# Block 2: projections woven with solve and scan together, hyena's two orders with the linear attention, its rows kept in SBUF, and the loop for large decays ahead of the solve

## The chip, the cores and the metric

The kernel runs on one NeuronCore of a Trainium2 chip. The core has a matrix engine (PE, with its weight loads as PEld), a vector engine (DVE), a scalar engine (ACT), GpSimd (POOL) and SyncE (SP), whose queue starts nearly all transfers here. Each engine works through its own instructions in order and waits for the others by semaphores. The metric is the device time of one execution in microseconds (us); the lower the better.

## What is computed

Two transformer blocks over one batch of 512 tokens of width 1024, in float32. Block 1 (RWKV-7 in both directions, neighbourhood attention, a mixture of experts) is not touched by the change. Block 2 takes block 1's output x and runs a mixer of three kinds of heads side by side, then an output projection and an MLP:

```python
def mixer(h, hc, ...):
    zl_hy, zl_gla, zl_gdn = split_last(h @ w_in, IN_SIZES)     # latent, 512 tokens
    zc_hy, zc_gla, zc_gdn = split_last(hc @ w_in, IN_SIZES)    # context, 256 tokens
    hy_lat = hyena_mix(zl_hy, ...)          # two long convolutions by FFT, each with a gate
    gla_lat, gla_ctx = gla_branch(zl_gla, zc_gla, ...)         # gated linear attention
    gdn_lat, gdn_ctx = gdn_branch(zl_gdn, zc_gdn, ...)         # gated delta rule
    y_lat = jnp.concatenate([hy_lat, gla_lat, gdn_lat], axis=-1) @ w_out

def hyena_mix(...):
    y = v
    for o, gate in enumerate((x1, x2)):
        conv = irfft(rfft(y, n=2 * l) * filt_f[None, :, o], n=2 * l)[:, :l]
        y = gate * (conv + d_skip[o] * y)

def gla_chunk_scan(q, k, v, log_a, s0):     # per chunk of 64 tokens
    b = jnp.cumsum(ac, axis=2)
    attn = einsum('bhid,bhjd,bhijd->bhij', qc, kc, exp(where(mask, b_i - b_j, -inf)))
    o = (qc * exp(b)) @ s + attn @ vc
    s_new = exp(b_last) * s + (kc * exp(b_last - b)).T @ vc

def gdn_chunk_scan(q, k, v, g, beta, s0):   # per chunk of 64 tokens
    a = -(kb @ kc.T) * exp(where(strict, diff, -inf))
    w, u = triangular_solve(eye - a, [kb * exp(gcum), vc * bc])
    v_new = u - w @ s
    o = (qc * exp(gcum)) @ s + attn @ v_new
    s_new = exp(g_last) * s + (kc * exp(g_last - gcum)).T @ v_new
```

Both scans run forward and backward over eight chunks of 64 tokens, four heads each, and the two directions are added. Each head's rows are then normalised (`gated_head_norm`), multiplied by a gate and go into the output projection. The context's part of the mixer is computed earlier in the kernel and leaves the starting states of the two scans.

## The kernel before

**Number format.** A float32 product is made of three matmuls on numbers split into a high and a low part: `mm3` (L293 to L295) issues high x high, low x high, high x low. The split is an ACT copy (L839, or L287 for weights) and a DVE subtraction (L840, L288).

**Weaving.** The order of the program is written by generators. `weave` (L331) takes streams with a weight each; a stream yields the cost of the piece that it has just written, and the stream with the least cost over weight writes next. A higher weight thus gives a stream more of the program for each piece of the others. All engines' instruction orders follow from it, through a scheduler that may move an instruction ahead where its inputs and buffers allow.

**Block 2's mixer, `mixer_in`.** In the order of the program:

- *Early.* `side_proj` (its loop at L1899) is a stream of projections of the latent: for each block of 128 columns 24 matmuls `gps` of 128x512 (8 pieces of the width, three each), then a store to DRAM. Its first nine blocks (`GDN_BLOCKS`: q, k, v of the delta rule) are written in `early()`, woven with `prep()`, which reads them back and lays them out, and with `gla_flags`, which finds whether any decay of the linear attention is too large for the fast form.
- *Solve.* `gdn_solve` makes, for each of two pairs of heads, decays and products (`dps`, `kkp`, `qkp`), and inverts the chunks' triangular matrices (`inverse`: a sum F to DRAM and back as n16, fifteen steps on DVE, to DRAM and back as qc, masked to qv, then 128 small matmuls `ips` and the result TQ). It is woven with all that is left of `side`, the other 20 blocks, weights 64 and 108. The projections' buffers are then given up (`far.close`).
- *Scan.* `gdn_scan` has eight chunks, one behind the other. In a chunk, for each head: `gxp` (key times state), gX on DVE, `gup` (TQ times gX), vd on DVE and vn on ACT, `gsp` (key times vd), the new state gSn on DVE; and the output `gop` with Og on ACT and DVE, stored to `ogd`. It is woven, 128 to 48, with `hy_tables` (loads and splits the DFT's tables) and `hyena(hp, 0)`: transposes `hyt`, forward DFT `dfp` (96 matmuls of 128x256 for an order), the filter's product on DVE and POOL, inverse DFT `hip` (48 matmuls of 128x512), and hv on DVE.
- *The loop for large decays.* `gla_general` reads the flag into registers (`TENSOR_LOAD aflag`, L1683) and runs its body 0 or 1 times; with the given data it is skipped. It would write the rows to `oad`, which else hold zeros.
- *Last stage.* `gla` is woven, 112 to 36 to 40, with the head norm of the delta rule's rows (`head_norm_out` on `ogd`) and `hyena(hp, 1)`, whose hv go to `mixd` in DRAM. For each chunk and pair of heads `gla` makes the output `aop` and the state's `asp`; the output is added to a piece of `oad` that is read into the tile Oa and written back (L1636 to L1638).

**`mixer_out`** begins with the head norm of `oad` (eight loads hO, `ops` that adds the directions, `otp` transposes), woven with `side()`: two blocks of hyena and three of the delta rule are read from `mixd` (`uld`), split into vh, vl and uh, ul, and multiplied with the output weights (`gpt`). The linear attention's three blocks come last.

## Time and profile before

| | us |
|---|---|
| median of 3 runs | 2232.9 |
| lowest and highest | 2223.94, 2236.71 |
| profiled execution | 2231.45 |
| its span | 2229.7 |
| mean granted clock of PE | 0.925 of full speed |

| engine | busy us | share of the span | instructions |
|---|---|---|---|
| PE | 1979.0 | 89% | 15280 |
| DVE | 1141.5 | 51% | 2542 |
| ACT | 718.0 | 32% | 1390 |
| POOL | 241.8 | 11% | 246 |

The stages that the change touches lie between about 1290 and 1845 us of the span: the early stage until 1417.5, the solve until 1537.3, the scan until 1654.8, the loop's stop until 1661.0, the last stage until 1756.5 (the last `aop`), the gap to the first `gpt` at 1778.8, then the output projection. All else is equal in both programs. Busy times are read by stage; a busy PE is not PE at its peak, since its matmuls overlap and get longer when the granted clock is low.

### The profile page before, as it was taken

To read this page: it belongs to the slowest core of one execution; us is meant where nothing else is said; L and a number is where in the kernel's file an instruction comes from. 1 tells how busy PE (TensorE), PEld (TensorE's weight loads), DVE (VectorE), ACT (ScalarE), POOL (GpSimd) and SP (SyncE) were. 2 spreads that over 40 slices of the span, in tenths; PEclk is the share of its full clock that TensorE was granted. 3 is DMA by queue.
4 is the path that set the end of the run, shared out by engine and by line. 5 is a ranking of instruction groups with operands and counts; after the bars stand their busy time and mean duration, and the time that the engine had idled before them with its cause. 6 is when DMAs were issued, how large, how long until landed. Compare 5 with 4: busy or idle time off the path is not lost. (4 is left out here: it accounts for less than half of the span.)

```text
span 2229.7 us, 37859 instructions
## 1 busy us (share of the span) xinstructions
PE 1979.0 (89%) x15280; PEld 1445.7 (65%) x15280; DVE 1141.5 (51%) x2542; ACT 718.0 (32%) x1390; POOL 241.8 (11%) x246
## 2 busy tenths in 40 slices
PE   7999999989688789999999487999989788999997
PEld 5777777657565675444534265776666486899897
DVE  4655555542136545454361487656547475433433
ACT  4333332312126343121322455423223124312321
POOL 0010000010000201111000031210001050000000
PEclk9999999986889988999999798998789799999998
DMA  5343222462555438978687432333123532333332
GB/s 152 105 99 106 63 87 56 129 188 87 187 173 174 156 113 294 315 299 291 256 312 261 170 113 89 101 107 114 39 66 119 169 107 91 92 96 92 94 94 76
DMA packets 183028, 319.54 MB, mean 143 GB/s; under 512 B 77896, under 2 KB 99161, under 8 KB 182843
## 3 DMA queue, kind: packets, MB, share of 16 engines
q1 hardware_dynamic: 175354, 303.38, 42.6%
q0 software_dynamic: 4608, 8.40, 1.1%
q10 hardware_dynamic: 2880, 5.24, 0.8%
q8 instruction: 122, 2.00, 0.4%
q14 instruction: 64, 0.52, 0.1%
HBM read 281.90 MB, written 43.44 MB: 146 GB/s over the span
## 5 line engine op out<-in xcount | busy, mean ns | idle before, releaser
L288 DVE TENSOR_TENSOR wl<-wraw,wh 128x1024 fp32r<-128x1024 f32 (+2 forms) x215 | 223.3, 1040 | 202.8 <-ACT wh L287 202.3
L287 ACT ACTIVATE wh<-wraw 128x1024 fp32r<-128x1024 f32 (+2 forms) x233 | 195.7, 844 | 284.4 <-PE gpt L326 149.1
L293 PE MATMUL gps<-hh,wh 128*128 128x512 f32 x568 | 234.1, 413 | 0.4 <-DVE rS L380 0.4
L295 PE MATMUL gps<-hl,wh 128*128 128x512 f32 x568 | 229.7, 405 | 0.0
L294 PE MATMUL gps<-hh,wl 128*128 128x512 f32 x568 | 229.1, 404 | 0.3 <-DVE wl L288 0.3
L1170 PE MATMUL hps<-w,xT 128*64 128x512 f32 x512 | 142.0, 612 | 1.7 <-DMA w<-in_w_moe 1.5
L324 PE MATMUL gpt<-wh,mh 128*128 128x256 f32 x512 | 142.9, 279 | 0.0
L325 PE MATMUL gpt<-wl,mh 128*128 128x256 f32 x512 | 142.9, 279 | 0.0
L326 PE MATMUL gpt<-wh,ml 128*128 128x256 f32 x512 | 142.9, 279 | 0.0
L293 PEld LDWEIGHTS gps<-hh,wh 128*128 128x128 f32 x568 | 108.2, 191 | 29.4 <-issue 3.9
L295 PEld LDWEIGHTS gps<-hl,wh 128*128 128x128 f32 x568 | 107.8, 190 | 25.1 <-issue 0.9
L294 PEld LDWEIGHTS gps<-hh,wl 128*128 128x128 f32 x568 | 108.0, 190 | 24.4 <-DVE wl L288 0.7
L294 PE MATMUL gps<-lhh,wl 128*128 128x512 f32 x232 | 96.8, 419 | 9.1 <-DVE wl L288 7.5
L293 PE MATMUL gps<-lhh,wh 128*128 128x512 f32 x232 | 95.7, 414 | 6.5 <-ACT cpad L1262 4.6
L325 PEld LDWEIGHTS gpt<-wl,mh 128*128 128x128 f32 x512 | 96.2, 188 | 0.1
L324 PEld LDWEIGHTS gpt<-wh,mh 128*128 128x128 f32 x512 | 96.2, 188 | 0.1
L326 PEld LDWEIGHTS gpt<-wh,ml 128*128 128x128 f32 x512 | 96.2, 188 | 0.0
L295 PE MATMUL gps<-lhl,wh 128*128 128x512 f32 x232 | 95.1, 412 | 0.2 <-DVE lhl L275 0.2
L1996 POOL TENSOR_TENSOR x<-x,xev 128x512 f32<-128x512 f32 x36 | 49.9, 1393 | 409.4 <-DVE xev L1994 406.4
L1170 PEld LDWEIGHTS hps<-w,xT 128*64 128x64 f32 x512 | 37.2, 138 | 64.0 <-issue 52.3
L324 PE MATMUL gpt<-wh,uh 128*128 128x256 f32 x224 | 66.1, 295 | 5.6 <-ACT wh L287 2.1
L1271 DVE SCALAR_TENSOR_TENSOR cout<-cpad,cw,cout 128x512 f32<-128x512 f32 (+1 forms) x90 | 68.6, 762 | 2.0
(1176 smaller groups left out, 4251.2 us busy)
## 6 DMA issues: line engine op xcount, KB each, us to landing
w<-in_w_moe SPq DMA_DIRECT2D x192, 512.0 KB
wraw<-in_w_modb SPq DMA_DIRECT2D x48, 512.0 KB
wraw<-in_w_in_2b SPq DMA_DIRECT2D x41, 512.0 KB
wraw<-in_w_inb SPq DMA_DIRECT2D x39, 512.0 KB
wraw<-in_w_mlp1b SPq DMA_DIRECT2D x32, 512.0 KB
wraw<-in_w_mlp2b SPq DMA_DIRECT2D x32, 512.0 KB
gd<-st SPq DMA_DIRECT2D x16, 256.0 KB
bm<-in_c_bias SPq DMA_DIRECT2D x16, 256.0 KB
```

The source lines that it names most:

```text
L287: nc.scalar.activation(wh, raw[:, o:o + g], AF.Copy)
L288: self.we.tensor_sub(wl, raw[:, o:o + g], wh)
L293: nc.tensor.matmul(ps, wh, hh, start=first, stop=False)
L294: nc.tensor.matmul(ps, wl, hh, start=False, stop=False)
L295: nc.tensor.matmul(ps, wh, hl, start=False, stop=last)
L324: nc.tensor.matmul(ps, hh[:, g, sl], wh[:, k], start=f, stop=False, skip_group_check=True)
L325: nc.tensor.matmul(ps, hh[:, g, sl], wl[:, k], start=False, stop=False, skip_group_check=True)
L326: nc.tensor.matmul(ps, hl[:, g, sl], wh[:, k], start=False, stop=l, skip_group_check=True)
L1170: nc.tensor.matmul(ps[q], xT[:, 4 * kh + k, q], self.parts[h][:, 512 * (k - 2 * c):512 * (k - 2 * c) + 512], start=kh == 0 and k == 0, sto ...
L1271: nc.vector.scalar_tensor_tensor(ov[:n], pv[:n, :, j:j + L], wcol[:n, j:j + 1], ov[:n], op0=OP.mult, op1=OP.add)
L1996: (nc.gpsimd if last is None or cb < 3 else nc.vector).tensor_add(o, o, t)
```

## The change

- `gla` adds its outputs to a slice of a tile that stays in SBUF, `self.oa` (1.5 MB), which is filled once from `oad` ahead of the stage. The 16 loads of Oa, the 16 stores, and the eight loads hO of the second head norm are gone. The tile's pool, `self.ox`, is closed in `mixer_out`, behind the head norm.
- `early()` runs through 16 blocks (the nine of the delta rule and seven of the linear attention) with weight 96 in place of nine with 54.
- `gla_general` stands right behind that, ahead of the solve.
- Solve and scan are one stream, `chain()`, woven 192 to 66 with the rest of the projections.
- `hy_tables`, both orders of hyena, `gla` and the delta rule's head norm are woven in one stage, 88 to 112 to 36; nothing of hyena is woven with the scan.

```diff
@@ -1632,10 +1632,8 @@
                             hh = 2 * hp + h
                             nc.tensor.matmul(op[t, h, :], attn[h][t, c, :], v[t, c, 96 * hh:96 * hh + 96], start=False, stop=h == 1,
                                              skip_group_check=True)
-                    O = pool.tile([128, 192], F32, name="Oa", bufs=3)
-                    nc.sync.dma_start(O, od[c, :, 192 * hp:192 * hp + 192])
+                    O = od[:, c, 192 * hp:192 * hp + 192]
                     nc.vector.tensor_add(O, O, op.rearrange("p h d -> p (h d)"))
-                    nc.sync.dma_start(od[c, :, 192 * hp:192 * hp + 192], O)
                 if c < S - 1 or ctx:
                     for z in range(2):
 
@@ -1921,7 +1919,7 @@
             self.there.add(n)
             yield 6
 
-    def head_norm_out(self, pool, od, gate, gcol, j0):
+    def head_norm_out(self, pool, od, gate, gcol, j0, O=None):
 
         nc, C = self.nc, self.C
         sgs = []
@@ -1930,9 +1928,10 @@
             nc.sync.dma_start(sg, self.sgd[gate + j])
             sgs.append(sg)
         yt = pool.tile([128, 4, 4, 96], F32, name="hyt")
-        O = pool.tile([128, 8, 384], F32, name="hO")
-        for c in (0, 7, 1, 6, 2, 5, 3, 4):
-            nc.sync.dma_start(O[:, c], od[c])
+        if O is None:
+            O = pool.tile([128, 8, 384], F32, name="hO")
+            for c in (0, 7, 1, 6, 2, 5, 3, 4):
+                nc.sync.dma_start(O[:, c], od[c])
         ss = pool.tile([128, 4, 4], F32, name="hss")
         for tt in range(4):
             ps = self.ps.tile([128, 384], F32, name="ops", tag="p", bufs=2)
@@ -2077,7 +2076,7 @@
 
         nc = self.nc
         tp = self.tc.tile_pool
-        self.far = ExitStack()
+        self.far, self.ox = ExitStack(), ExitStack()
         w = self.w = self.view(dict(p="g", s="g", i="p"), wg=512)
         cx, w.wraw, w.wsp = [self.far.enter_context(tp(name=n, bufs=b, side="right"))
                                    for n, b in (("lat", 1), ("wr3", 2), ("ws3", 2))]
@@ -2124,37 +2123,40 @@
                             st[hp] = yield from v.gdn_kv(hp, 8, gd, gt, src, hp)
 
                 def early():
-                    while not w.there.issuperset(GDN_BLOCKS):
+                    while not w.there.issuperset(SIDE_BLOCKS[:16]):
                         yield next(side)
                 with tp(name="gf", bufs=1) as gf:
-                    self.run(self.weave((early(), 54), (prep(), 60), (v.gla_flags(8, gf), 20)))
+                    self.run(self.weave((early(), 96), (prep(), 60), (v.gla_flags(8, gf), 20)))
+                with tp(name="gz", bufs=1) as ga:
+                    v.gla_general(8, ga, lambda n: load(ga, self.gpd[n], "lsc"), self.oad)
 
                 with tp(name="gs", bufs=1) as gs, tp(name="rp2", bufs=1) as v.rp:
                     heads = []
 
-                    def solve():
+                    def chain():
                         with tp(name="gs2", bufs=1) as tmp, tp(name="ri2", bufs=1) as v.ri:
                             for hp in range(2):
                                 kv, kT = st[hp]
                                 E, TQ = yield from v.gdn_solve(hp, 8, gs, tmp, st["g"], kT, st["q"], hp)
                                 heads.extend((2 * hp + e, kT[:, e], st["q"][:, 2 * hp + e], kv[:, :, e], kv[:, :, 2 + e], E[:, e], TQ[e])
                                              for e in range(2))
+                        yield from v.gdn_scan(8, gs, heads, st["g"], self.ogd)
                     next(side)
-                    self.run(self.weave((solve(), 64), (side, 108)))
+                    self.run(self.weave((chain(), 192), (side, 66)))
                     self.far.close()
+                    self.oa = self.ox.enter_context(tp(name="oa", bufs=1, side="right")).tile([128, 8, 384], F32, name="oa")
+                    nc.sync.dma_start(self.oa, self.oad.rearrange("c p d -> p c d"))
                     hp = self.far.enter_context(tp(name="hy", bufs=1, side="right"))
                     u = self.view(dict(p="g", s="g", i="g"))
 
-                    def hyena0():
+                    def hyena():
                         yield from u.hy_tables(hp)
                         yield from u.hyena(hp, 0)
-                    self.run(self.weave((v.gdn_scan(8, gs, heads, st["g"], self.ogd), 128), (hyena0(), 48)))
-            with tp(name="gz", bufs=1) as ga:
-                v.gla_general(8, ga, lambda n: load(ga, self.gpd[n], "lsc"), self.oad)
+                        yield from u.hyena(hp, 1)
             with tp(name="ga", bufs=1) as ga, tp(name="hn", bufs=1) as hn:
                 un = self.view(dict(p="i"))
-                self.run(self.weave((v.gla(8, False, ga, lambda n: load(ga, self.gpd[n], "lsc"), self.oad), 112),
-                                    (un.head_norm_out(hn, self.ogd, 0, self.gng, 5), 36), (u.hyena(hp, 1), 40)))
+                self.run(self.weave((v.gla(8, False, ga, lambda n: load(ga, self.gpd[n], "lsc"), self.oa), 112),
+                                    (un.head_norm_out(hn, self.ogd, 0, self.gng, 5), 36), (hyena(), 88)))
             self.far.close()
 
     def mixer_out(self, xs, x, ev):
@@ -2181,7 +2183,8 @@
                     self.gemm_tm("w_out_2b", cb, uh[:, 3:], ul[:, 3:], 4, ev(cb), 1, 1, nk=3)
                     yield 4
             with tp(name="hn", bufs=1) as pool:
-                self.run(self.weave((self.head_norm_out(pool, self.oad, 3, self.agng, 2), 18), (side(), 28)))
+                self.run(self.weave((self.head_norm_out(pool, None, 3, self.agng, 2, self.oa), 18), (side(), 28)))
+            self.ox.close()
             for k in range(3):
                 take(2 + k, uh[:, k], ul[:, k])
             for cb in range(4):
```

What this does to the order of instructions, at the three places where most is moved:

PE, a chunk in the middle of the scan, before. kT, kv, TQ and E are keys, keys and values, inverses and products of the delta rule; dh, dl, di with hs0 and hs1 are hyena's tables and spectra:

```order
L294 MATMUL hip<-dh,hs0l 128x512
L295 MATMUL hip<-dl,hs0h 128x512
L1469 MATMUL gup<-gX,TQ_13339 64x96 x2
L293 MATMUL hip<-di,hs1h 128x512
L294 MATMUL hip<-di,hs1l 128x512
L295 MATMUL hip<-dl,hs1h 128x512
L293 MATMUL hip<-di,hs1h 128x512
L1469 MATMUL gup<-gX,TQ_13358 64x96 x2
L294 MATMUL hip<-di,hs1l 128x512
L1483 MATMUL gsp<-vd__14994,kv_12156 96x96
```

The same place after, a chunk late in the scan:

```order
L1494 MATMUL gop<-gSn,qT__12177 64x96 x4
L1459 MATMUL gxp<-gSn,kT_12863 64x96 x2
L1469 MATMUL gup<-gX,TQ_13841 64x96 x2
L1469 MATMUL gup<-gX,TQ_13860 64x96 x2
L1483 MATMUL gsp<-vd__14880,kv_12360 96x96 x2
L1469 MATMUL gup<-gX,TQ_14219 64x96 x2
L1496 MATMUL gop<-vn__14882,E_13484 64x96 x2
```

The 128x512 matmuls of hyena are gone from between the scan's own; no projections stand in their place here. Of all 696 `gps` matmuls 353 stand ahead of the solve's first matmul before and 444 after, 343 and 228 from there to the last `ips`, none and 24 behind it.

PE at the skipped loop, before: what stands ahead of it are hyena's forward DFTs of order 1.

```order
L293 MATMUL dfp<-yth,dh 128x256 x2
L294 MATMUL dfp<-yth,dl 128x256 x2
L295 MATMUL dfp<-ytl,dh 128x256 x2
L293 MATMUL dfp<-yth,dh 128x256
L1683 TENSOR_LOAD aflag
L1684 COMPARE_AND_BRANCH
```

After, at the end of the early stage; `tcp` are transposes of the preparation:

```order
L1373 MATMUL tcp<-ct_58,kv_12692 96x128 x8
L295 MATMUL gps<-lhl,wh 128x512
L293 MATMUL gps<-lhh,wh 128x512
L294 MATMUL gps<-lhh,wl 128x512
L295 MATMUL gps<-lhl,wh 128x512
L1681 TENSOR_LOAD aflag
L1682 COMPARE_AND_BRANCH
```

The branch moved from between scan and last stage to between early stage and solve.

SP's queue from the end of the last stage on, before: Oa and hO are the linear attention's rows, x the residual, uld what the output projection reads.

```order
L1636 DMA Oa<-oad 128x192 x2
L1935 DMA hO<-oad 128x384 x3
L1638 DMA oad<-Oa 128x192 x2
L1935 DMA hO<-oad 128x384
L225 DMA g1r<-mdd 128x1024
L1987 DMA x_16742<-x1d 128x1024 x4
L1935 DMA hO<-oad 128x384
L2170 DMA uld<-mixd 128x512 x2
```

The same place after; hsg are the gates of the head norm, wraw the output weights:

```order
L1885 DMA mixd<-hv_15572 128x512
L1885 DMA mixd<-hv_15573 128x512
L225 DMA g1r<-mdd 128x1024
L1986 DMA x_16699<-x1d 128x1024 x4
L1928 DMA hsg_16717<-sgd 128x512
L1928 DMA hsg_16719<-sgd 128x512
L1928 DMA hsg_16721<-sgd 128x512
L2172 DMA uld<-mixd 128x512 x2
```

The rows' reads and writes are gone, and hyena's last two stores now stand shortly ahead of the uld that reads them.

## Rows read from the trace of the kernel before

**Rows 1.** Busy time by stretch: start:end, us, each engine, PEclk, DMA share, GB/s.

```profile
1369.00:1398.00 29.00, 20.56 (x86) 15.19 (x87) 17.90 (x52) 18.05 (x34) 2.57 (x6) 0.82 0.37 118
1417.50:1537.30 119.80, 112.01 (x1136) 90.16 (x1134) 79.55 (x151) 29.46 (x51) 21.39 (x23) 0.98 0.36 100
1537.30:1654.80 117.50, 113.66 (x782) 76.56 (x781) 65.55 (x232) 36.23 (x104) 6.50 (x8) 0.77 0.19 60
1661.00:1756.50 95.50, 87.78 (x775) 65.42 (x776) 60.39 (x146) 29.30 (x55) 11.93 (x10) 0.87 0.38 119
1756.50:1778.80 22.30, 11.89 (x31) 3.53 (x30) 2.48 (x5) 4.08 (x9) 0.00 (x0) 0.77 0.73 254
...
1537.20:1546.85 9.65, 7.62 (x70) 4.92 (x66) 6.29 (x26) 2.65 (x8) 0.00 (x0) 0.90 0.74 222
```

In each of these rows the five busy times are those of PE, PEld, DVE, ACT and POOL, with the number of instructions.

**Rows 2.** Timeline of PE, two neighbouring projection matmuls: start, us, engine, line, operation.

```profile
1410.02 0.39 PE L294 MATMUL gps<-lhh,wl 128*128 128x512 f32 x1
1410.25 0.39 PE L295 MATMUL gps<-lhl,wh 128*128 128x512 f32 x1
```

**Rows 3.** Timeline of PE behind the skipped loop; idle time before it in brackets.

```profile
1661.01 0.58 PE L294 MATMUL dfp<-yth,dl 128*128 128x256 f32 x1 [5.58 <-issue]
```

**Rows 4.** The solve: PE's costliest group, then DVE's timeline.

```profile
L294 PE MATMUL gps<-lhh,wl 128*128 128x512 f32 x115 | 46.8, 407 | 4.8 <-DVE wl L288 4.8
...
1473.06 0.68 DVE L702 TENSOR_TENSOR TQ<-ips,qv 128x512 f32<-128x512 f32 x1
1492.06 1.07 DVE L649 TENSOR_REDUCE F<-Nw 128x128 f32<-128x512 f32 x1
1536.59 0.69 DVE L702 TENSOR_TENSOR TQ<-ips,qv 128x512 f32<-128x512 f32 x1 [0.24 <-PE ips L682]
```

**Rows 5.** Waits of DVE in the scan: us in total, times, longest.

```profile
DVE gSn L1486 <- PE gsp L1483: 24.9, 32, 2.7
```

**Rows 6.** The line of gxp: count, ns min/median/max, first and last start.

```profile
L1459 PE MATMUL gxp<-gSn,kT x112: 246/297/423, 1541.6 to 1648.8; 96*64 96x96 f32 x112
```

**Rows 7.** Timeline of DVE, the first gX of chunks 0 and 1.

```profile
1537.19 0.31 DVE L1462 TENSOR_SCALAR gX<-gxp,eG 128x96 f32<-128x96 f32 x1
1546.85 0.31 DVE L1462 TENSOR_SCALAR gX<-gxp,eG 128x96 f32<-128x96 f32 x1
```

**Rows 8.** Hyena: PE's timeline, DVE's groups in the scan, DVE's timeline.

```profile
1661.61 0.41 PE L293 MATMUL dfp<-yth,dh 128*128 128x256 f32 x1
1661.82 0.41 PE L294 MATMUL dfp<-yth,dl 128*128 128x256 f32 x1
...
1665.10 0.28 PE L294 MATMUL dfp<-yth,dl 128*128 128x256 f32 x1
1665.22 0.28 PE L295 MATMUL dfp<-ytl,dh 128*128 128x256 f32 x1
...
L840 DVE TENSOR_TENSOR dl<-hraw,dh 128x512 fp32r<-128x512 f32 x8 | 5.3, 683 | 0.8 <-ACT dh L839 0.8
L1885 DVE TENSOR_TENSOR hv<-hv,hx 128x512 f32<-128x512 f32 x2 | 1.4, 680 | 0.0
...
1647.53 0.68 DVE L1885 TENSOR_TENSOR hv<-hv,hx 128x512 f32<-128x512 f32 x1
1737.20 0.68 DVE L1885 TENSOR_TENSOR hv<-hv,hx 128x512 f32<-128x512 f32 x1
```

**Rows 9.** The gap: timelines of DVE and PE, then the chain: start, us, what.

```profile
1757.63 0.67 DVE L1637 TENSOR_TENSOR Oa<-Oa,aop 128x192 f32<-128x192 f32 x2 [2.20 <-DMA Oa<-oad]
1772.07 0.90 PE L1943 MATMUL ops<-hO,ct 128*64 128x384 f32 x1 [4.61 <-DMA hO<-oad]
1778.83 0.39 PE L324 MATMUL gpt<-wh,vh 128*128 128x256 f32 x1 [1.51 <-ACT wh L287]
...
1809.79 4.90 DMA uld<-mixd
1819.92 3.27 DMA uld<-mixd
```

## Prediction

> **What bounds the kernel now.** I read the busy time by stage first [rows 1], because the share of busy time over the whole span mixes stages with different limits. The change touches five stages of block 2, and the reader should see in [rows 1] that each has its own limit. The tail of the early stage (1369.0 to 1398.0 us) is loose: PE works 20.56 of 29.00 us, at a granted clock of 0.82. The solve (1417.5 to 1537.3) is PE's: 112.01 of 119.80 us busy at 0.98, DVE only 79.55. The scan (1537.3 to 1654.8) looks like PE's too, 113.66 of 117.50, but at a clock of 0.77: its matmuls take long, and hyena's large ones stand among the scan's small ones. The last stage before the output projection (1661.0 to 1756.5) has PE at 87.78 of 95.50. The gap behind it (1756.5 to 1778.8) is a wait for memory: PE 11.89 of 22.30, DVE 2.48.
>
> Then the waits of DVE inside the scan [rows 5]: the state update gSn waits 24.9 us, 32 times, for its own matmul gsp. The scan is a serial chain PE, DVE, PE, DVE, and PE works in order. The instruction order of before shows hip matmuls between gup and gsp, so the chain's next matmul comes behind them. The rows of two gX [rows 7] show what a chunk costs where hyena is still thin: the first gX of chunk 0 starts at 1537.19, that of chunk 1 at 1546.85, so 9.66 us, against 117.5 / 8 = 14.7 us on the mean.
>
> The profiled execution took 2231.45 us, 1.45 less than the median of the runs shown. The sum is made against it, and 1.45 is added at the end.
>
> **Early stage: +11.** The instruction order has 353 projection matmuls (gps, of 696) ahead of the solve's first matmul before, and 444 after: 91 more. Two neighbours start 0.23 us apart [rows 2], so 91 x 0.23 = 20.9 us of PE work comes into this stage. The loose stretch has 29.00 - 20.56 = 8.4 us of idle PE in it, and a clock of 0.82; were it full, the 20.56 us of work there would take up to 3.7 less, of which I take 1.5. So 20.9 - 8.4 - 1.5 = +11. Bounds: 0, if the blocks spread under all of the preparation, and +20.9, if none of it is hidden.
>
> **Loop for large decays: 0.** Its body is skipped, but PE stood still 5.58 us for it [rows 3]; it now does so between the early stage and the solve. The instruction is the same and is taken once in both programs, and in both places PE has work waiting. Bounds: -5.6, if PE's projections and preparation run out under it, and +5.6, if the solve's start now waits for a second engine's branch. [...]
>
> **Solve: -26.** PE is the bound. It holds 344 projection matmuls now, three lines of 115 or so, one of which is the first row of [rows 4]; the order of after leaves 228 there (91 go ahead, 24 are woven with the scan). 115 or 116 fewer x 0.23 = 26.5 us. A look at the chain says the same can be had: from TQ of the first pair of heads (1473.06) to F of the second (1492.06) are 19.0 us [rows 4], in which the second pair's decays and products are made; after has both pairs' fronts at the stage's start, and of the 19 I leave 4 for Nw and F, a saving of 15, and the inverse's 128 ips matmuls stand in a row where gps lay between them (44.5 us from F to TQ, 1492.06 to 1536.59, should lose some 10). Bounds 0 (the chain of inverses keeps its length and only PE's idle grows) and -30.
>
> **Scan: -47.** Only 24 gps are woven with it, all else that lay between leaves. A chunk then costs what [rows 7] show less the two hyena splits on DVE in that window, of which one lies on DVE's path: 9.66 - 0.7 (a dl takes 683 ns [rows 8]), about 8.9, and x 8 = 71 against 117.5, so -47. Below: DVE was busy 6.29 us in that window [rows 1], 1.37 of it the two splits, so 4.9 us a chunk is the floor; I take the middle of 4.9 and 9.66, 7.3 us a chunk, 58 for the stage, -59. Above: 0, if 14.7 us is the chain's own length.
>
> **Last stage (gla, head norm, now both orders of hyena): +36.** Here the work of hyena's order 0 comes back. PE: 96 dfp matmuls at 0.12 us (1665.10 and 1665.22 [rows 8]) make 11.5, 48 hip of 128x512 at 0.23 (the same shape [rows 2]) make 11.0, and some 20 dfp of order 1 that before had ahead of the loop make 2.4: 24.9 us, on an engine that is busy 92% of the stage. DVE: order 0 has eleven groups of hyena work in the scan, from dl (5.3 us) to hv (1.4) [rows 8], 22.6 us in all. DVE is busy 60.39 of 95.50, so I put half on the path: 11.3. Sum 36.2, the stage 131.5 us. Bounds: 24.9 less PE's idle 7.7, +17, and 24.9 + 22.6 = +47; the first rival goes further.
>
> **Rows kept on chip: -14.** Before, the gap of 22.3 us [rows 1] is a chain through memory: Oa is read (DVE waits 2.20 us for it, 1757.63), added, written, and read again as hO, for which PE waits 4.61 us until 1772.07; the first gpt starts at 1778.83 [rows 9]. After, the head norm's ops and 12 transposes stand ahead of all gpt and take their rows from the chip, and what must pass through memory is hyena's last mixd, read back as uld. Such a read is 4.90 us where the chain shows it [rows 9]; with the store ahead of it, the split and the first weights (1.51 us [rows 9]) I take 13 us for the gap: -9. In the output projection the chain has two waits for uld, 4.90 and 3.27 us; these reads no longer stand behind the rows' reads and writes on SP's queue, and I take 5 of the 8.2. Bounds: -4 and -22. The 1.5 MB read of the rows ahead of the stage has the whole of gla's decays in front of its first use, hence nothing; uncovered it would cost 6 us, at the 254 GB/s of the gap [rows 1]. The reads and writes of Oa and hO (40 DMA issues on SP) end on no other engine's path than these.
>
> **Sum:** 11 + 0 - 26 - 47 + 36 - 14 = -40. 2231.45 - 40 = 2191.5, with 1.45 to the median 2193.
>
> **Rivals.** A, the slower one: *hyena is a chain of its own and keeps its pace.* Its order 0 ran from the scan's start, 1537.3, to hv at 1647.5 + 0.7 = 1648.2, 110.9 us; order 1 from there to 1737.9, 89.7 less the 6.2 of the loop's stop, 83.5 [rows 8]. One behind the other these are 194 us in the last stage instead of 131.5: +63, 2256. For it: each order is a line of split, transform, filter, inverse, split, and while the scan runs alone hyena doesn't move at all. Against it: PE was held by the scan's and gla's matmuls in both stretches, and the weight of hyena rises from 48 of 176 and 40 of 188 to 88 of 236. Gain ends where the stage takes over 171 us; it is slower by over 0.5% (11.2 us, about what a measurement of this kernel can tell) from 183.
>
> B, same: *the scan's 14.7 us are its own.* Its waits are on its own matmuls [rows 5]. Then +47: 2240. Against it stands the first chunk.
>
> C, same: *the projections only change places.* Early pays its 20.9 in full (+9.9) and the solve keeps its length (+26): 2229. For it: the two inverses stay one behind the other, since the second pair's Nw and F follow the first's TQ in the order; against it, PE's 112 of 119.8.
>
> D: *PE falls to its lower clock in the lone scan.* [...]
>
> E: *more overlap.* The last stage adds PE's time only (+24.9, 11 less) and the scan falls to 58 us (13 less): 2193 - 24 = 2169.
>
> That the change doesn't do what it says is in the sum: the projections are hardly woven with the scan, 24 of 252 matmuls.
>
> **How the numbers follow.** Chances: the forecast 0.50, E 0.10, D 0.12, C 0.12, B 0.06, A 0.10. Of D three quarters fall under 2221.7, the bound for faster. Faster 0.50 + 0.10 + 0.09 = 0.69; same 0.12 + 0.06 + 0.03 = 0.21; slower 0.10. The range of 2155 to 2240 leaves out A and the ends of E and B, under 2 in 10. The likeliest case, faster, has 2165 to 2221 for its own.
>
> **What would show it.** Right: a scan of 65 to 75 us with gSn's wait for gsp well under 24.9; a solve of 90 to 98; first dps matmul 10 to 12 us later than 1417.5 with the loop's stop of some 5.6 ahead of it; a stage of 125 to 140 from the scan's end to the last aop or hv; under 14 us from there to the first gpt. Wrong: a last stage over 171 us, with DVE and PE both idle while hyena's splits wait for each other (A); chunks of 14 us with nothing between them (B); a solve of 115 with an idle PE (C); a clock under 0.7 in the scan and the stage behind (D).

## The result and the profile after

The changed kernel takes 2201.42 us (median of 4 runs, 2197.05 to 2206.44) against 2228.61 us before (4 runs): ratio 0.986, 95% interval 0.9826 to 0.9895, so 27 us less. The forecast was 40 less. The profiled execution has a span of 2197.8 us against 2229.7, 31.9 less, and this is where they are:

| stretch of the trace | before | after | difference | forecast |
|---|---|---|---|---|
| first latent projection to the solve's first matmul | 154.8 | 175.2 | +20.4 | +11, and the loop's stop |
| solve, to the end of the last TQ | 119.7 | 96.5 | -23.2 | -26 |
| scan, to the end of the last Og | 117.5 | 87.7 | -29.8 | -47 |
| last stage, to the end of the last aop | 101.8 | 119.6 | +17.8 | +36, less the loop's stop |
| gap to the first gpt | 22.3 | 14.7 | -7.6 | -9 |
| output projection, to the MLP's first transpose | 70.8 | 62.4 | -8.4 | -5 |
| all else | 1642.8 | 1641.8 | -1.0 | 0 |

The busy times after by stage (columns as in [rows 1]) answer to [rows 1]:

```profile
1437.39:1533.87 96.48, 89.15 (x1060) 71.15 (x1059) 74.71 (x152) 23.09 (x42) 20.05 (x23) 0.97 0.33 89
1533.87:1621.53 87.66, 84.55 (x596) 53.77 (x595) 45.97 (x177) 20.32 (x63) 0.00 (x0) 0.66 0.15 50
1621.53:1741.17 119.64, 111.63 (x958) 85.25 (x957) 78.71 (x194) 45.38 (x95) 19.77 (x18) 0.95 0.31 99
1741.17:1755.86 14.69, 6.81 (x35) 4.07 (x35) 8.73 (x27) 6.02 (x12) 0.00 (x0) 0.79 0.90 321
1755.86:1818.22 62.36, 48.91 (x387) 47.55 (x385) 47.00 (x67) 20.43 (x51) 32.13 (x22) 0.91 0.49 153
```

Read the clock in the second row: 0.66 in the scan, where the forecast had taken its chunk at 0.90. Cut chunk by chunk (from the first gX of one to that of the next, chunks 1 to 7), the scan after reads:

```profile
1538.40:1552.20 13.80, 13.80 (x90) 8.48 (x87) 6.69 (x27) 2.19 (x7) 0.00 (x0) 0.86 0.04 15
1552.20:1571.03 18.83, 18.83 (x90) 11.13 (x88) 6.35 (x25) 2.51 (x8) 0.00 (x0) 0.50 0.03 10
1571.03:1579.87 8.84, 8.79 (x71) 5.69 (x69) 5.08 (x22) 2.81 (x8) 0.00 (x0) 0.74 0.56 181
1579.87:1587.68 7.81, 7.56 (x82) 4.86 (x80) 5.75 (x26) 2.55 (x8) 0.00 (x0) 1.00 0.14 50
1587.68:1598.00 10.32, 10.32 (x80) 6.78 (x78) 5.98 (x25) 2.51 (x8) 0.00 (x0) 0.58 0.06 21
1598.00:1611.76 13.76, 12.31 (x86) 8.15 (x84) 8.30 (x30) 2.51 (x8) 0.00 (x0) 0.50 0.04 16
1611.76:1621.60 9.84, 8.48 (x74) 5.78 (x74) 5.15 (x20) 3.94 (x12) 0.00 (x0) 0.50 0.53 153
```

Two chunks of the same work, 82 and 80 records of matmuls, take 7.81 us at a clock of 1.00 and 10.32 at 0.58. The clock is not all that differs between chunks: the last two, both at 0.50, take 13.76 and 9.84 us. Chunk 0 is not in the rows: its four gX (L1462) stand in the solve now, at 1471.6 us, so that only 4.5 us of it lie behind the last TQ. The wait that the forecast named [rows 5] is still there, 18.0 us instead of 24.9 (waits of DVE in the scan: us, times, longest):

```profile
DVE gSn L1486 <- PE gsp L1483: 18.0, 29, 1.5
```

The loop's stop stands ahead of the solve now, as [rows 3] did behind the scan (PE's timeline; the wait in brackets):

```profile
1429.65 0.39 PE L295 MATMUL gps<-lhl,wh 128*128 128x512 f32 x1
1435.94 0.80 PE L293 MATMUL gps<-lhh,wh 128*128 128x512 f32 x1 [5.91 <-DVE gt L1417]
...
1437.39 1.05 PE L1419 MATMUL dps__13488<-gt,ct 128*128 128x512 f32 x1
```

The bracket names a DVE operation, gt, but the projection does not read it. Most of the stop is one branch of PE's own sequencer, 4.15 us, where the kernel before has one of 3.74 us (the loop's line after, then before: ns min/median/max, first and last start). Twelve waits for semaphores follow it, until 1435.65:

```profile
L1682 PEldq EVENT_SEMAPHORE  x13: 51/51/51, 1430.1 to 1435.6; - x13
L1682 PEldq COMPARE_BRANCH  x3: 70/183/4149, 1429.3 to 1435.7; - x3
...
L1684 PEldq COMPARE_BRANCH  x3: 70/196/3741, 1655.1 to 1660.8; - x3
```

In the solve the inverse's matmuls now come without a break. On DVE (timeline) from qv to the first pair's TQ are under 10 us, and the second F follows at once, where before 19.0 us lay between TQ and F [rows 4]:

```profile
1477.18 1.22 DVE L671 TENSOR_TENSOR qv<-qc,ct 128x1024 f32<-128x1024 f32 x1 [2.72 <-DMA qc<-qd]
...
1486.88 0.68 DVE L702 TENSOR_TENSOR TQ<-ips,qv 128x512 f32<-128x512 f32 x1
1487.48 1.48 DVE L709 TENSOR_TENSOR Nw<-gN,ct 128x512 f32<-128x512 f32 x1
1488.88 2.02 DVE L649 TENSOR_REDUCE F<-Nw 128x128 f32<-128x512 f32 x2
...
1533.18 0.69 DVE L702 TENSOR_TENSOR TQ<-ips,qv 128x512 f32<-128x512 f32 x1 [0.24 <-PE ips L682]
```

At the gap PE no longer waits for hO (PE's timeline, beside [rows 9]):

```profile
1752.51 1.95 PE L1956 MATMUL otp<-ct,hyt 128*128 128x128 f32 x8 [6.80 <-DMA uld<-mixd]
...
1755.86 0.78 PE L324 MATMUL gpt<-wh,vh 128*128 128x256 f32 x2
1758.85 0.58 PE L325 MATMUL gpt<-wl,vh 128*128 128x256 f32 x1 [2.22 <-DVE wl L288]
```

The bracket at the transposes `otp` names the read of hyena's rows, but they read hyt, the head norm's rows, which DVE's chain of small steps delivers just ahead of them. The read of uld ends about 1 us after they have begun: ACT, which splits it, waits until 1753.54, and the first gpt follows ACT's splits of it and of the weights (timelines of DVE and ACT):

```profile
1751.75 1.97 DVE L1952 TENSOR_TENSOR hyt<-hyt,hny 128x384 f32<-128x384 f32 x4
...
1753.54 1.31 ACT L839 ACTIVATE vh<-uld 128x512 fp32r<-128x512 f32 x2 [5.75 <-DMA uld<-mixd]
```

### The profile page after: what moved, and what is told of

It is laid out like the page before. It is cut to its first block, busy times and chain, and to the rows that moved or that the text cites. A ratio compares the mean times of both kernels' runs of the same rounds, so it can differ in the third digit from the quotient of the medians.

```text
span 2197.8 us, 37785 instructions
## 1 busy us (share of the span) xinstructions
PE 1956.7 (89%) x15280; PEld 1434.4 (65%) x15280; DVE 1140.1 (52%) x2542; ACT 719.4 (33%) x1390; POOL 241.4 (11%) x246
## 5 line engine op out<-in xcount | busy, mean ns | idle before, releaser
L288 DVE TENSOR_TENSOR wl<-wraw,wh 128x1024 fp32r<-128x1024 f32 (+2 forms) x215 | 228.5, 1065 | 201.6 <-ACT wh L287 201.0
L293 PEld LDWEIGHTS gps<-hh,wh 128*128 128x128 f32 x568 | 108.0, 190 | 29.8 <-issue 3.9
L294 PEld LDWEIGHTS gps<-hh,wl 128*128 128x128 f32 x568 | 107.8, 190 | 24.1 <-DVE wl L288 0.7
L2011 DVE TENSOR_TENSOR uld<-uld 128x512 f32<-128x512 f32 x32 | 22.1, 692 | 87.3 <-ACT uld L2010 87.3
```

The source lines that it names most:

```text
L288: self.we.tensor_sub(wl, raw[:, o:o + g], wh)
L293: nc.tensor.matmul(ps, wh, hh, start=first, stop=False)
L294: nc.tensor.matmul(ps, wl, hh, start=False, stop=False)
L2011: nc.vector.tensor_mul(f, f, f)
```

## Experiments

All ratios are to the kernel before, with 95% intervals. The stage lengths come from one profiled execution of each kernel, cut at the same events as above; "tail" is gap and output projection together. The part ahead of the first latent projection, which no edit touches, takes 1249.6 to 1264.9 us in these profiles, so spans are compared with care: a difference of some us between two of them can lie there.

| kernel | ratio | early | solve | scan | last | tail | span |
|---|---|---|---|---|---|---|---|
| before | 1 | 154.8 | 119.7 | 117.5 | 101.8 | 93.1 | 2229.7 |
| after | 0.986 (0.9826 to 0.9895) | 175.2 | 96.5 | 87.7 | 119.6 | 77.1 | 2197.8 |
| rows only | 0.993 (0.9898 to 0.9962) | 155.8 | 120.8 | 122.8 | 102.5 | 75.2 | 2212.9 |
| loop late | 0.992 (0.989 to 0.9949) | 168.4 | 96.1 | 94.8 | 135.1 | 77.2 | 2209.9 |
| no loop | 0.9868 (0.9809 to 0.9927) | 168.2 | 96.9 | 92.9 | 122.2 | 76.6 | 2195.9 |
| scan with hyena | 0.9973 (0.993 to 1.0016) | 174.1 | 118.5 | 116.3 | 98.8 | 75.1 | 2223.1 |
| scan alone | 0.9966 (0.9934 to 0.9997) | 174.5 | 119.8 | 86.0 | 118.5 | 77.1 | 2220.3 |
| old weights | 0.9946 (0.9911 to 0.9981) | 174.8 | 120.1 | 86.0 | 117.8 | 77.3 | 2214.4 |
| early nine | 0.9958 (0.9927 to 0.9989) | 159.6 | 87.0 | 108.7 | 143.3 | 77.0 | 2213.6 |
| old projections | 0.9929 (0.99 to 0.9959) | 158.3 | 121.2 | 83.8 | 122.7 | 76.6 | 2202.3 |
| float32 filler | 1.012 (1.0061 to 1.0178) | 174.1 | 121.0 | 125.8 | 114.5 | 77.4 | 2242.1 |
| filler of the projections' format | one run | 173.9 | 121.2 | 126.8 | 130.8 | 77.2 | 2274.4 |
| no outputs | one run | 176.5 | 118.7 | 71.6 | 116.2 | 77.3 | 2198.4 |
| tables in the scan | 0.9998 (0.9973 to 1.0023) | 176.6 | 93.7 | 131.7 | 111.9 | 75.0 | 2230.3 |

**Rows only.** The kernel before with the one part:

```diff
-                    O = pool.tile([128, 192], F32, name="Oa", bufs=3)
-                    nc.sync.dma_start(O, od[c, :, 192 * hp:192 * hp + 192])
+                    O = od[:, c, 192 * hp:192 * hp + 192]
                     nc.vector.tensor_add(O, O, op.rearrange("p h d -> p (h d)"))
-                    nc.sync.dma_start(od[c, :, 192 * hp:192 * hp + 192], O)
...
+            nc.sync.dma_start(self.oa, self.oad.rearrange("c p d -> p c d"))
```

> The kernel before with one part of the change alone: gla's rows stay in a tile on chip. Theory: the tail's gain of the change (gap 22.3 to 14.9 us, output projection up to the MLP 70.8 to 62.4) is this part's alone, and gla's DVE no longer waits for Oa (5.9 us in the last stage), of which a little comes on top: 16 to 20 us, ratio to before 0.991 to 0.993. Rival: the tail gains because the head norm and hyena end in another order in the changed kernel, and the reads of Oa and hO were hidden: under 6 us, ratio over 0.997.

The tail goes from 93.1 to 75.2 us, all of the changed kernel's gain there and 1.9 more; the span is 16.8 shorter, of which 7.2 lie ahead of the first latent projection, and the timed runs are 15.6 us shorter (0.993). The theory holds for the tail. That gla no longer waits for Oa gave nothing: the last stage is 102.5 against 101.8.

**Loop late, and no loop.** The changed kernel with `gla_general` moved back behind the scan, and without it:

```diff
-                with tp(name="gz", bufs=1) as ga:
-                    v.gla_general(8, ga, lambda n: load(ga, self.gpd[n], "lsc"), self.oad)
...
+            with tp(name="gz", bufs=1) as ga:
+                v.gla_general(8, ga, lambda n: load(ga, self.gpd[n], "lsc"), self.oad)
+            nc.sync.dma_start(self.oa, self.oad.rearrange("c p d -> p c d"))
```

> The changed kernel with the loop for large decays back between scan and last stage (the rows are loaded right behind it). Theory: the stop of PE of some 6 us is paid once in either place, so the time is that of the changed kernel within 3 us, ratio to before 0.985 to 0.988; the solve then starts some 6 us earlier and a stop of 5.5 to 6.2 us stands ahead of the last stage. Rival 1: ahead of the solve the stop also holds up DVE's chain and costs more than behind the scan: this one is 3 to 6 us faster, 0.983. Rival 2: in the old place all engines are empty and it costs more: 3 to 6 us slower, 0.989.

> The changed kernel without the loop for large decays, which leaves out the case of a large decay that the given data don't have. Theory: the stop ahead of the solve, 5.9 to 6.2 us and the wait for the first decays behind it, falls away: early 6 to 9 us shorter, all else within 3 us, ratio to before 0.982 to 0.984. Rival: the loop is also a wall that no instruction passes, and without it the solve's start slips in among the preparation: 10 us or more shorter, under 0.982.

Theory fell in the first: with the loop late the kernel is 12 us slower in the span and 0.992 in time. Its second rival had the direction, with 3 to 6 us. The early stage and the solve of the two kernels here agree within 0.8 us; with the loop late the last stage is 12.9 us longer, for a stop of 5.63. PE's timeline with the loop late shows the rest:

```profile
1616.94 0.59 PE L1496 MATMUL gop<-vn__14824,E 64*64 64x96 f32 x4
1623.16 1.12 PE L1850 MATMUL hyt<-ct,hv 128*128 128x128 f32 x4 [5.63 <-issue]
...
1634.41 1.97 PE L1290 MATMUL ttp<-ct,cfb 128*128 128x128 f32 x8 [4.06 <-DVE cfb L1279]
1638.76 1.54 PE L1941 MATMUL ops<-hO,ct 128*64 128x384 f32 x2 [2.38 <-DMA hO<-ogd]
```

and the same seam without the loop:

```profile
1616.23 0.59 PE L1496 MATMUL gop<-vn__14824,E 64*64 64x96 f32 x4
1617.20 0.66 PE L1850 MATMUL hyt<-ct,hv 128*128 128x128 f32 x2 [0.39 <-issue]
```

Behind the scan, the stop is followed by 4.06 and 2.38 us of waiting for what gla and the head norm could not fetch or lay out ahead of it. But these two kernels do not differ by the loop alone. With the loop late, the 1.5 MB read of the rows (oa) also stands behind the stop, ahead of gla's and the head norm's reads on SP's queue; without the loop it is issued in the scan, under other work (SP's timeline with the loop late, then without the loop):

```profile
1624.19 0.41 SPq L2155 DMA_DIRECT2D oa<-oad  x1
1624.65 0.71 SPq L2097 DMA_DIRECT2D lsc<-gv0d  x1
1633.92 0.32 SPq L2097 DMA_DIRECT2D lsc<-gv2d  x1
...
1562.43 0.37 SPq L2146 DMA_DIRECT2D oa<-oad  x1
```

At the 254 GB/s of [rows 1] this read alone takes an estimated 6 us. How the 12.9 us are shared between stop and read is not shown.

Ahead of the solve the loop costs 7.0 us of the early stage (175.2 against 168.2). The kernel without the loop should thus have been 7 us faster than the changed one. It is 1.9 shorter in its span, all of it ahead of the first latent projection, and equal in time: its scan is 5.2 and its last stage 2.6 longer, at a clock of 0.59 and 0.92 against 0.66 and 0.95 (scan and last stage without the loop, columns as in [rows 1]).

```profile
1524.56:1617.49 92.93, 90.16 (x596) 57.63 (x595) 46.39 (x177) 20.18 (x63) 0.00 (x0) 0.59 0.14 47
1617.49:1739.68 122.19, 115.47 (x958) 88.17 (x956) 78.58 (x194) 45.56 (x94) 19.54 (x18) 0.92 0.30 97
```

So loop and read in their new place bring 12 us of span against loop late; against no loop the loop's own price is lost among the clock's changes.

**Scan with hyena, and scan alone.** The changed kernel with the middle of before, and with a scan that has nothing beside it:

```diff
-                    self.run(self.weave((chain(), 192), (side, 66)))
+                    self.run(self.weave((solve(), 64), (side, 108)))
+                    self.run(v.gdn_scan(8, gs, heads, st["g"], self.ogd))
```

> The changed kernel with the weaving of before in the middle: solve with all that is left of the projections, scan with the tables and hyena's order 0, last stage with order 1 alone. Theory, from the two traces' stages: solve +5 us (24 projection matmuls more), scan 88 to 117 (+30), last stage 119 to 95 (-24): 11 us slower than the changed kernel, ratio to before 0.991. Rival: hyena costs the same wherever it stands, and the gain is that of the other parts: within 3 us of the changed kernel, 0.985 to 0.988.

> The changed kernel with the solve woven with all that is left of the projections, and the scan with nothing. Theory P (the 24 projection matmuls in the scan hold up its chunks 1 and 2, 13.8 and 18.8 us where others take 7.8 to 10): solve +5 us, scan 88 to about 72, 8 to 10 us faster than the changed kernel, ratio 0.982. Theory K (the chunks follow PE's granted clock, which is low in a scan that has nothing large beside it, 0.50 in chunks of 13.8 us and 1.00 in one of 7.8): the clock stays near 0.5, chunks of 10 to 14 us, scan 85 to 100 us, time equal or up to 15 us slower, 0.986 to 0.993.

The two kernels here differ by the place of hyena's tables and order 0 alone. Scan and last stage take 116.3 and 98.8 us with them in the scan, 86.0 and 118.5 with them behind: 10.6 less in sum. The timed runs, 0.9973 and 0.9966, are 1.6 us apart, well within their intervals, so they do not show that gain. For the scan alone theory K is right in its stage: without any projection the scan takes 86.0 us, 1.7 less than with 24 of them, at a clock of 0.53. Its time, 0.9966, lies outside K's range.

Both are far slower than expected because of the solve. It took 118.5 and 119.8 us, not the 102 of the forecast's 0.23 us a projection, although it held 252 of them against the 343 of before. PE was busy 95.96 of 119.78 us:

```profile
1439.26:1559.04 119.78, 95.96 (x1083) 77.14 (x1081) 75.97 (x155) 24.03 (x43) 21.33 (x23) 0.88 0.32 87
1559.04:1645.09 86.05, 84.28 (x578) 54.81 (x578) 44.74 (x177) 21.91 (x67) 0.00 (x0) 0.53 0.13 42
```

The second row is the lone scan. In these two kernels the solve had before's weights, 64 and 108. So the next three kernels take the projections apart.

**Old weights, early nine, old projections.** The changed kernel with one and then both of before's settings for the projections:

```diff
-                    self.run(self.weave((chain(), 192), (side, 66)))
+                    self.run(self.weave((chain(), 64), (side, 108)))
...
-                    while not w.there.issuperset(SIDE_BLOCKS[:16]):
+                    while not w.there.issuperset(GDN_BLOCKS):
...
-                    self.run(self.weave((early(), 96), (prep(), 60), (v.gla_flags(8, gf), 20)))
+                    self.run(self.weave((early(), 54), (prep(), 60), (v.gla_flags(8, gf), 20)))
```

> The changed kernel with the weights of before for the weaving with the projections: chain 64, side 108 in place of 192 and 66; solve and scan are still one stream. Theory O (the solve's length is set by where the chain's matmuls stand among the projections, and not by how many projections PE has): as with the scan alone, the solve goes back from 96.5 to 118 to 121 us though it has only 252 of the 344 projections of before, the scan stays at 84 to 92, ratio to before 0.994 to 0.998. Theory N (PE's work sets it, 0.23 us a projection): 26 more projections than in the changed kernel, 102 us, ratio 0.988.

> The changed kernel with the early stage of before (nine blocks, weight 54): 335 projection matmuls ahead of the solve, 207 in it, 153 with the scan. Theory: early 12 to 16 us shorter, solve as in the changed kernel (94 to 98), and the scan takes the 129 more at 0.23 to 0.47 us each on an engine that is its bound, +30 to +60: 15 to 45 us slower than the changed kernel, ratio 0.993 to 1.006. Rival: the scan has room for projections, and these raise the granted clock: scan within 15 us of 87.7, time as the changed kernel's or less, ratio 0.980 to 0.986.

> The changed kernel with both of before's settings for the projections: nine blocks and weight 54 in the early stage, chain 64 against side 108 (360 projection matmuls in the solve, none in the scan). Theory O (with these weights the solve takes some 120 us whether it holds 252 projections or 344, so the 15 us that seven blocks more cost the early stage are given away unless the weights change as well): early 158 to 162, solve 118 to 126, scan 86, last stage 118: within 8 us of the changed kernel, ratio to before 0.985 to 0.991. Theory N (the two settings are worth what each lost when it was undone alone, 17 and 16 us): some 33 us slower than the changed kernel, 1.000 or more.

With the old weights the solve takes 120.1 us with 252 projections and 121.2 with 360: 108 matmuls more cost 1 us. With the new ones it takes 96.5 us with 228. What the weights change is where the chain's matmuls stand. With the old weights, and 252 projections, DVE's timeline has 16 us from the first W to the last TQ of the first pair, where the changed kernel has 5 (1481.79 to 1486.88 on the same events):

```profile
1489.74 1.28 DVE L693 TENSOR_TENSOR W<-ips,qv 128x512 f32<-128x512 f32 x2
...
1506.14 0.68 DVE L702 TENSOR_TENSOR TQ<-ips,qv 128x512 f32<-128x512 f32 x1
```

and PE then stands for want of anything else (waits of PE in the solve):

```profile
PE ips L682 <- DVE qv L671: 17.7, 1, 17.7
```

Theory O holds in the solve of both. With the new weights the amount is not without effect: with nine early blocks the solve holds 207 projections, 21 fewer, and takes 87.0 us, 9.5 less, where 94 to 98 had been expected, on a PE that is nearly always busy:

```profile
1418.18:1505.21 87.03, 82.94 (x1031) 65.92 (x1031) 65.27 (x133) 21.63 (x39) 20.90 (x13) 0.98 0.39 104
```

Still this kernel loses: its early stage is 15.6 us shorter, but 153 projections stand behind the solve, the scan grows by 21.0 and the last stage by 23.7.

With both old settings together the span is only 4.5 us longer than the changed kernel's, while each alone makes it some 16 longer. In the timed runs that kernel stands at 0.9929, some 15 us behind the changed one, outside the range that theory O gave (0.985 to 0.991); the two kernels with one old setting are 19 and 22 behind. Its profiled execution, 2204.22 us, is the third fastest of its 12 runs, whose median is 2210.46, so the 4.5 us are probably too few.

This kernel has the rows on chip and both moves, of the loop and of hyena, but the old projections. Its 0.9929 is what rows only reaches (0.993). So the timed runs show the gain in two parts, each some 15 us: the rows on chip, and the projections' two settings taken together. They show none from the two moves, within the intervals of some 7 us either way; the profiles have 10.6 us between the spans of these two kernels.

**What bounds the lone scan.** Two fillers and one omission, all on the kernel with the scan alone:

```diff
+                    fl = self.ps.tile([96, 256], F32, name="fil", tag="g", bufs=2)
+                    nc.tensor.matmul(fl, X[i], E.rearrange("p c t -> p (c t)")[:, :256], start=True, stop=True)
...
+                    xr = pool.tile([128, 96], F32R, name="xr", bufs=2)
+                    nc.scalar.activation(xr, X[i], AF.Copy)
...
+                for z in range(2 if self.fill is not None else 0):
+                    fl = self.ps.tile([96, 512], F32, name="fil", tag="g", bufs=2)
+                    nc.tensor.matmul(fl, xr, self.fill[:, z], start=True, stop=True)
...
-                        nc.tensor.matmul(op[q, 0], qT[:, c, q], So[i][:, d], start=True, stop=True)
-                        nc.tensor.matmul(op[q, 1], E[q, c, :], vn[i][q], start=True, stop=True)
```

> The kernel with the scan alone, plus 32 idle matmuls of 128x256 float32 in the scan, one a head and chunk, that nobody reads (about 0.43 us each at the higher clock, 14 us in all, estimated from the 128x512 ones of the solve at 0.9 to 1.0 us). Theory K (the lone scan is slow since PE's clock is low, because there is nothing large in it): the granted clock goes from 0.53 to over 0.8 and the scan, 86.0 us without them, takes 72 to 82 us. Rival: the clock stays near 0.5 and the matmuls come on top at 0.85 us: 100 to 115 us.

> The kernel with the scan alone, plus 64 idle matmuls of 96x512 in the format of the projections (two a head and chunk, 0.23 us apart at the higher clock) and 32 small ACT copies. The projections and hyena's matmuls are of this format; the idle ones of the filler tried above were float32. Theory K2 (the large matmuls of the projections' format bring the clock up): granted clock in the scan over 0.8, scan 70 to 85 us against 86.0. Rival: the clock stays near 0.53 and they come on top at 0.43 us or more: 105 to 120 us.

> The kernel with the scan alone, without the scan's output matmuls gop (four of the ten matmuls of a head and chunk; ACT and DVE work on vn instead, so the mixer's output is not the reference's). Theory PE (the lone scan is a row of small matmuls on PE at the lower clock, and whatever is put in or taken out of the row counts in full): 86.0 us become 52 to 62. Theory chain (the four steps of the state, PE to DVE and back, set the length, and the outputs fill gaps): 76 to 86 us.

The scan's stretch in the three, in this order:

```profile
1544.67:1670.44 125.77, 125.47 (x634) 72.11 (x634) 49.02 (x186) 27.57 (x77) 0.00 (x0) 0.54 0.13 42
...
1560.01:1686.77 126.76, 125.18 (x626) 70.72 (x626) 43.77 (x174) 26.81 (x88) 0.00 (x0) 0.51 0.06 18
...
1553.55:1625.17 71.62, 58.83 (x346) 37.76 (x346) 46.73 (x184) 23.66 (x72) 0.00 (x0) 0.52 0.18 59
```

Neither filler raised the clock: 0.54 and 0.51 against 0.53. Of the fillers 28 of the 32 float32 matmuls and 56 of the 64 of the projections' format lie in these stretches, the rest in the solve (a float32 matmul has two records here: [rows 6] have 112 for the 56 gxp of seven chunks):

```profile
L1475 PE MATMUL fil<-E,gX 128*96 128x256 f32 x56 | 32.4, 685 | 0.1
L1480 PE MATMUL fil<-lhh,xr 128*96 128x512 f32 x56 | 34.9, 698 | 0.4 <-ACT xr L1471 0.4
```

They lengthen the scan by 39.8 and 40.8 us, 1.4 and 0.7 each, more than either rival had said, so PE had no room. Both theories of a clock that comes up with large matmuls beside the scan fell. (The last stage of the second is 12.3 us longer than with the scan alone, at a clock of 0.89 in its first 112.5 us; why is open.) Without the outputs the scan takes 71.6 us, between the two expectations: 14.4 us less where PE is busy 25.5 less. So at this clock the scan without outputs is some 70 us long, with PE busy 82% of it, and the outputs' matmuls add about half of their time. It is one run.

**Tables in the scan.** The changed kernel with hyena's tables loaded and split beside the scan:

```diff
-                    self.run(self.weave((chain(), 192), (side, 66)))
+                    self.run(self.weave((solve(), 192), (side, 66)))
...
+                    self.run(self.weave((v.gdn_scan(8, gs, heads, st["g"], self.ogd), 128), (u.hy_tables(hp), 16)))
```

> The changed kernel with the solve alone woven 192 to 66 with the projections, the buffers given up behind it, and the scan woven 128 to 16 with the loads and splits of hyena's tables, which have no matmul; the rest as in the changed kernel. Theory: solve 95 to 99 as in the changed kernel, since its weight is the same; the splits lie under a scan that PE bounds (84 to 90 us), and the last stage starts with the tables there, 2 to 5 us shorter: ratio to before 0.981 to 0.985. Rival: the splits stand in DVE's order ahead of the chain's steps, scan 92 to 98: no gain, 0.986 to 0.989.

The solve confirms the weights once more: 93.7 us with 233 projections. The scan takes 131.7, far beyond the rival's 98. With the tables there early, the scheduler put most of hyena's first transforms into the scan (PE's groups of the scan), and they ran slowly, 0.48 to 0.52 us of record each at a clock of 0.53, against 0.28 [rows 8] at 1.00. Their 42 us of PE are nearly all of the 44 that the scan is longer:

```profile
L293 PE MATMUL dfp<-yth,dh 128*128 128x256 f32 x29 | 13.9, 479 | 0.0
L294 PE MATMUL dfp<-yth,dl 128*128 128x256 f32 x29 | 13.9, 479 | 0.0
L295 PE MATMUL dfp<-ytl,dh 128*128 128x256 f32 x28 | 14.4, 522 | 0.0
```

The last stage got 7.7 us shorter for 44 more in the scan. None of these versions beats the changed kernel.

## Why the prediction was right, and where its steps were not

The direction and the range hold, and each stage moved the way that was forecast. The sum, -40 against -32 in the trace and -27 in the timed runs, hides misses of both signs, so that it came this near is in part luck. Of the lengths named as signs of being right only the solve's came as said: 96.5 us, in 90 to 98. The scan (87.7, forecast 65 to 75), the first dps matmul (19.9 us later, forecast 10 to 12), the last stage (119.6, forecast 125 to 140) and the gap (14.7, forecast under 14) are outside, and D's sign, a clock under 0.7 in the scan, came: 0.66.

- **Rows on chip: right, also in its size.** -14 forecast, -16.0 after, -17.9 alone. One half of the split was not: the waits for uld in the output projection did not shrink (7.2 us in two waits before, 8.6 in three after). That stage is 8.4 us shorter with 48.91 us of PE against 54.46 and 47.00 of DVE against 54.16; that the head norm's transposes and their work are done ahead of it explains this, but was not tried alone.
- **Solve: right number, wrong reason.** The step "PE is the bound, 115 or 116 fewer x 0.23" failed. It read 112.01 of 119.80 us busy as a bound. The experiments with 252 projections and the old weights kept 120 us with PE idle a fifth of the time. The new weights and the order that they make are what bring the gain: with them alone undone the solve is back at 120.1 us. Of the second estimate, from the chain, the larger half was right: the 19.0 us from TQ to the second pair's F went down to some 3. The other half was not: from that F to the last TQ it is still 43 to 44 us, where some 10 of 44.5 were to go. The other gain is the first pair's: from the first dps matmul to its TQ 49.5 us in place of 55.5.
- **Early stage: near.** Without the loop it is 168.2 us, 13.4 more than before, for +11. Rival C said that the projections only change places. For the two settings of the projections this is nearly what happened: together they are worth 4.5 us in the profile, and some 15 in the timed runs. C's condition, a solve that keeps its length, didn't come true because of the weights.
- **Loop: the step "0" was wrong.** Ahead of the solve it costs the early stage 7.0 us; behind the scan, loop and the uncovered read of the rows together cost the last stage 12.9. That PE's stop itself is the same in the two places was right: 5.58 us [rows 3] and 5.91. The forecast left out what follows the stop: behind the scan three streams begin there, and their reads stand behind it, and behind the 1.5 MB, on SP's queue. Of the stop 3.74 us behind the scan and 4.15 ahead of the solve are one branch of PE's sequencer; why that branch takes so long is not shown.
- **Scan: mis-sized by 17 us, -47 for -29.8.** The term took 8.9 us for a chunk from a stretch with a clock of 0.90 and used it for all eight. Chunks 1 to 7 take 83.2 us after, 11.9 each; chunk 0 takes only 4.5, since its start slipped into the solve. The longer chunks are those at a lower clock or with projections: 7.81 us at 1.00, 10.32 at 0.58, 13.76 at 0.50, 18.83 at 0.50 with 8 projections in it. Rival D had the low clock. No run shows the price by which three quarters of it were put under 2221.7: in the runs the whole chunk of some 80 records of matmuls is longer, 10.32 us at 0.58 against 7.81 at 1.00, and the last stage is back at 0.95. That the hyena matmuls stood in the chain's way was right: 116.3 us with them, 86.0 without. Rival B is out with that.
- **Last stage: mis-sized the other way.** Its +36 was 24.9 us of PE and 11.3 of DVE. On the forecast's own stretch, without the loop's stop, the stage grew by 24.1 us (95.5 to 119.6), and between scan with hyena and after it grows by 20.8 us and PE's busy time by 21.5. DVE's half of 22.6 us does not show, as rival E had it for this stage. Rival A, with hyena as a chain of its own at 194 us, is out.

## What to carry to other kernels

A stage in which an engine is 94% busy is not shown to be bound by it: if its filler can be placed earlier or later, take a third of the filler out and see whether the stage shrinks. Here the order of a chain's small matmuls among the filler was worth 24 us, and the amount of filler 1 in the poor order; in the good one, 21 matmuls fewer went with 9.5 us less. The price of a runtime loop or branch is not its stop alone (here 5.91 us, and 7.0 in the stage): look at what begins right behind it and must wait for its reads. Before two kernels are called different by one thing, look for what else moved with it, as the read of the rows did with the loop. A wait's named releaser is an inference: check that the waiting instruction reads what it names. A duration read at one granted clock was not that at another (a dfp matmul of before took 0.28 us at 1.00 and 0.41 at 0.50 [rows 8]): before multiplying it by a count, look up the clock of the stretch that it will run in.

## What the runs showed of the hardware

The lone scan keeps PE busy 98% of its time in the records and has a granted clock of 0.53. Read us by us, the changed kernel's scan stands at 1.00 until 1548 and from 1576 to 1589, and at 0.50 from 1549 to 1575 and from 1590 to its end; only the three us of a change have other values, 0.64 to 0.68. What brings the clock down is not shown. By the records PE hardly waited in the lone scan, busy for 84.28 of 86.05 us, and not at all in a chunk of 18.83 us at 0.50. Whether such a busy time, made of many short matmuls, hides gaps is not shown either. Idle matmuls of 128x256 float32 or 96x512 in the projections' format, 28 and 56 of them in the scan, left it at 0.54 and 0.51. In one chunk of the changed kernel's scan it was 1.00. What made it rise there, and in before's scan (0.77), is open.
